# The first norm of a two-block kernel: transposed by products with a diagonal of roots, weighted piece by piece per partition

## The chip, the cores and the metric

The kernel runs on one core of a Trainium2 chip. The metric is the time of one execution in microseconds (us) of device time; lower is better. All data is fp32. Five engines work side by side, each through its own queue in order: TensorE (PE, with its weight loads shown apart as PEld), VectorE (DVE), ScalarE (ACT), GpSimd (POOL) and SyncE (SP), which here only issues DMAs.

## The reference

Two transformer blocks follow each other on x of 256 rows and 1,024 columns. The change touches only the beginning of the first layer: the first RMS norm and the projection that reads it.

```python
def rms_norm(x, w):
    y = x * lax.rsqrt(jnp.mean(x * x, axis=-1, keepdims=True) + NORM_EPS)
    return y * w

for layer in range(2):                      # first block
    h = rms_norm(x, norm_w[layer])
    proj = h @ w_in[layer]                  # q, k, v, z, q_h, f_h, i_h, g_h, two gates
    ...                                     # HGRN recurrence, windowed attention, merge
    x = x + merged @ w_out[layer]
x = rms_norm(x, final_norm_w)
...                                         # second block: attention, convolution, MoE, PLE
```

## The kernel before, in words

**Exact products from split parts.** Every fp32 factor of a projection is kept as a high part (fp32r) and a low part (the rest). `mm3` makes one product from three matmuls: high·high (L380), low·high (L381) and high·low (L382), all into one accumulator (`acc`).

**Weights.** They lie in one DRAM array, `w_all`, in units of 1 MB in the order of use, and are streamed by `Stream` into three buffers `raw`. Each unit is cut in two halves; `prepare` makes of a half its high part `whi` (ACT, L287) and its low part `wlo` (DVE, L288). A unit's DMA can go out when the buffer it takes has been split. Two units belong to the job "f", the next two to the job "i", then come those of "qh".

**The first norm.** x has two tiles of 128 rows (t = 0, 1). For each, `MeanRoot` squares the two halves on ACT (L509), adds and scales on DVE (L514, L496) and takes the root on POOL (L497). `norm_scale` (L525) multiplies x by its root and by the norm's row of weights `wb`, which a DMA has spread over all 128 partitions. `transpose_split` turns eight blocks of 128 columns on PE (L565, four to one PSUM tile `tr` of 128x512, 2 KB a partition), and `split_to` (L555) makes from each PSUM tile the high part `hTh` (ACT) and the low part `hTl` (DVE), 512 columns in one instruction each. `kk` counts the eight blocks of 128 columns of h, which are the eight steps of the contraction.

**The first projection.** `rows_job` runs "f" and then "i": each has four halves of weights, each half two steps kk, each step three matmuls of 512 columns for each row tile. That is 48 matmuls for "f", 48 for "i", 96 together, before "qh" begins. In order it does two halves for tile 0, then the same two for tile 1.

**Order.** Engines run their queues in order. A scheduler places instructions by priority when the program is built; `ahead` shifts the priority and `issue_after` ties one instruction behind another. `warm_up` issues PE products of zeros at the start (12 passes of 256 columns) and behind the first transposes (6 passes).

Of the kernel before, what the change touches and what calls it, by code (L numbers as in the profile page):

```python
# [9 lines left out]
F32 = mybir.dt.float32  # L10
F32R = mybir.dt.float32r
I32 = mybir.dt.int32
AF = mybir.ActivationFunctionType
OP = mybir.AluOpType
# [4 lines left out]
DM = 1024  # L19
KT = DM // 128  # L20
# [38 lines left out]
class Weights:  # L59


    def __init__(self):
        self.parts, self.units, self.off = [], [], 0
# [77 lines left out]
@contextmanager  # L141
def ahead(g, n):

    tc = g.tc
    tc.cur_priority -= n
    g.off += n
    yield
    g.off -= n
    tc.cur_priority += n
# [170 lines left out]
class Lazy:  # L320
# [5 lines left out]
    def __call__(self):  # L326
        if self.tile is None:
            self.tile = self.make()
        return self.tile
# [52 lines left out]
    nc.tensor.matmul(out, al, bh, start=False, stop=last)  # L382


def rows_job(g, specs, act, n, nk=KT, per=None, tile_first=False):

    hT, lT = act.hi, act.lo
    per = per or max(1, min(1024 // n, nk // 2))
    nh = nk // per

    def part(t, ps, j, hi, lo):
        s = slice(t * 128, (t + 1) * 128)
        for k in range(per):
            kk = j * per + k
            mm3(g, ps[:, :n], (hT[:, kk, s], lT[:, kk, s]), (hi[:, k], lo[:, k]), kk == 0, kk == nk - 1)

    if tile_first:
        held = {}
        for t in range(2):
            for tag, evac in specs:  # L400
                ps = g.acc.tile([128, 512], F32, tag="acc", name="acc")
                for j in range(nh):
                    while t not in act.have:
                        yield WAIT
                    if t == 0:
                        held[tag, j] = g.st.take(tag, n)
                    i, hi, lo = held[tag, j]
                    part(t, ps, j, hi, lo)
                    if t:
                        g.st.free(i)  # L410
                    if j == nh - 1:
                        with ahead(g, -10):
                            evac(t, ps)
                    yield
    else:
        for tag, evac in specs:
            while len(act.have) < 2:
                yield WAIT
            ps = [g.acc.tile([128, 512], F32, tag="acc", name="acc") for _ in range(2)]
            for jj in range(0, nh, 2):  # L420
                held = {}
                for t in range(2):
                    for j in range(jj, min(jj + 2, nh)):
                        if t == 0:
                            held[j] = g.st.take(tag, n)
                        i, hi, lo = held[j]
                        part(t, ps[t], j, hi, lo)
                        if t:
                            g.st.free(i)
                        if j == nh - 1:  # L430
                            with ahead(g, -10):
                                evac(t, ps[t])
                        yield
# [29 lines left out]
def start(g, n_keep):  # L463
    nc, h = g.nc, g.h
    g.st = Stream(g)
    g.fl = Filler(g)
    g.x = [g.keep.tile([128, DM], F32, name=f"x{t}") for t in range(2)]
    g.const = g.keep.tile([128, n_keep], F32, name="const")
    o, n = g.at["ident"]
    nc.sync.dma_start(out=g.x[0], in_=h["x"][0, 0:128, :])  # L470
    nc.scalar.dma_start(out=g.const[:, o:o + n], in_=h["const"][:, o:o + n])

    def c(name, n=0):
        o, k = g.at[name]
        return g.const[:, o:o + (n or k)]

    g.c = c
    g.half = g.keep.tile([128, 8], F32, name="half")
    nc.vector.memset(g.half, -0.5)

    g.zero = t4(g, "zero")[:, 0]
    nc.gpsimd.memset(g.zero, 0.0)
    warm_up(g, 6)


def warm_up(g, n):

    ps = g.sm.tile([128, 512], F32, tag="s", name="warm")
    for i in range(n):
        g.nc.tensor.matmul(ps[:, 0:256], g.zero[:, 0:128], g.zero, start=True, stop=True)  # L490
# [9 lines left out]
class MeanRoot:  # L500
# [5 lines left out]

    def half(self, c):
        s = slice(c * 512, (c + 1) * 512)
        self.g.nc.scalar.activation(self.scr[:, s], self.x[:, s], AF.Square, accum_out=self.ss[:, c:c + 1])  # L509

    def end(self):
        g, ss = self.g, self.ss
# [3 lines left out]
        return r  # L516


def norm_scale(g, x, wb, h, r, behind=None):

    nc = g.nc
    with g.tc.issue_after(behind.ins) if behind is not None else ExitStack():
        for c in range(2):
            s = slice(c * 512, (c + 1) * 512)
            nc.vector.scalar_tensor_tensor(h[:, s], x[:, s], r, wb[:, s], op0=OP.mult, op1=OP.mult)  # L525


def double_norm(g, x, wf, wb):
# [43 lines left out]
def normed(g, wb, hT, before):  # L572

    fl = g.fl
    h = [None] * 2
    mr = [None] * 2

    def squares(t):
        h[t] = t4(g, "h", shape=(128, DM))
        mr[t] = MeanRoot(g, g.x[t], h[t])  # L580
        for c in range(2):
            mr[t].half(c)

    def rest(t, fill, behind=None):
        norm_scale(g, g.x[t], wb, h[t], mr[t].end(), behind)
        for b in (0, 4):
            if fill:
                fl.fill((4 if b else 6) if t else 3)
            last = transpose_split(g, h[t], hT, t, b, b + 4)
        return last  # L590

    if before is None:
        for t in range(2):
            squares(t)
        last = rest(0, False)
        warm_up(g, 3)
        g.st.after(*last)
        g.st.prepare(1)
        g.st.after()
        return rest(1, False, last[1])  # L600
    for t in range(2):
        if t:
            fl.until(before)
        squares(t)
        last = rest(t, True)
    return last


def load_row(g, tag, src, n=DM):
    t = g.p.tile([128, n], F32, tag=tag, name=tag, bufs=g.nwb if tag == "wb" else 1)  # L610
    g.nc.sync.dma_start(out=t, in_=bcast(src))
    return t
# [46 lines left out]
def t2(g, name, dt=F32, shape=(128, 512)):  # L659
    return g.p.tile(list(shape), dt, tag="t2", name=name, bufs=g.nt2)  # L660


def t4(g, name, dt=F32, shape=(128, 4, 256)):
    return g.mid.tile(list(shape), dt, tag="t4", name=name, bufs=g.nt4)
# [22 lines left out]
def first_block(g):  # L687
    nc, h, p, fl = g.nc, g.h, g.p, g.fl
    g.nt2, g.nwb = 4, 2
    wb = load_row(g, "wb", h["norm_w"][0])  # L690
    nc.sync.dma_start(out=g.x[1], in_=h["x"][0, 128:256, :])
    last = None
    for l in range(2):
        last = first_layer(g, l, wb, last)
        wb = load_row(g, "wb", h["norm_w"][1] if l == 0 else h["final_norm_w"])
    return last, wb


def lower_bound(g):

    nc, h, p = g.nc, g.h, g.p
    e = t2(g, "lbe", shape=(128, 4, 128))[0:4, 0:2]
    m = g.lbr = p.tile([4, 128], F32, name="lbr")
    for l in range(2):
        nc.sync.dma_start(out=e[:, l], in_=h["lb_logits"][l].rearrange("(a d) -> a d", d=128))
    nc.vector.tensor_max(m, e[:, 0], e[:, 1])
    nc.vector.tensor_sub(e, e, m.unsqueeze(1).to_broadcast([4, 2, 128]))
    nc.scalar.activation(e, e, AF.Exp)
    nc.vector.tensor_add(m, e[:, 0], e[:, 1])
    nc.vector.reciprocal(m, m)  # L710
    nc.vector.tensor_mul(e, e, m.unsqueeze(1).to_broadcast([4, 2, 128]))
    nc.vector.tensor_add(m, e[:, 0], e[:, 1])
    nc.vector.tensor_sub(m, m, e[:, 0])
# [15 lines left out]
def first_layer(g, l, wb, last):  # L729
    nc, h, p, fl = g.nc, g.h, g.p, g.fl  # L730
# [54 lines left out]
    if l:  # L785
        jf = fl.add(rows_job(g, [("f", evac_f), ("i", evac_i)], hT, 512, tile_first=True))
    else:
        jf = fl.add(rows_job(g, [("f", evac_f), ("i", evac_i)], hT, 512))
    jqh = fl.add(cols_job(g, "qh", hT, 512, evac_qh))
    jq = fl.add(rows_job(g, [("q", evac_q)], hT, 512))  # L790
    jkv = fl.add(rows_job(g, [("kv", evac_kv)], hT, 256))
# [11 lines left out]
    fl.until(jf)  # L803
    if l == 0:
        first_setup(g)
        lower_bound(g)
    g.st.bufs, g.st.slack = 6, 1

    bT.hi, bT.lo = t4(g, "bTh", F32R), t4(g, "bTl", F32R)
# [861 lines left out]
def host_arrays(inputs):  # L1671
    inputs = {k: np.asarray(v) for k, v in inputs.items()}
    ws = lay_out(**{n: inputs[n] for n in _WEIGHTS})
    const, at, n_keep = constants()
    arrays = {n: np.ascontiguousarray(inputs[n]) for n in _SMALL}
    arrays["w_all"] = np.concatenate(ws.parts)
    arrays["const"] = const
    arrays["conv_w"] = np.ascontiguousarray(
        inputs["conv_w_2"][0].reshape(3, 4, 128).transpose(2, 0, 1).reshape(128, 12))
    route = np.concatenate([inputs["w_rg_2"][0], inputs["w_re_2"][0]], 1)  # L1680
    arrays["w_route"] = np.ascontiguousarray(route.reshape(KT, 128, 20).transpose(1, 0, 2).reshape(128, KT * 20))
    return arrays, ws.units, at, n_keep
# [15 lines left out]
```

## Time and profile before

| | |
|---|---|
| median of 3 runs | 764.17 us (762.84 to 764.51) |
| the profiled execution | 762.69 us |
| its span, from first to last instruction | 760.9 us |
| PE busy | 744.0 us (98%) |
| DVE, ACT, POOL busy | 450.1, 350.1, 21.8 us |
| TensorE clock granted by the throttle | 1.00 of full speed |

The span is what the rows of a trace cover; the execution is 1.8 us longer than it. Times inside the trace count from the span's start. PE is busy nearly all the time, so the table says only that what delays PE is what costs; where PE is not busy has to be read by stretch.

### The profile page before, as it was taken

To read this page: it belongs to the slowest core of one execution; us is meant where nothing else is said; L and a number is where in the kernel's file an instruction comes from. 1 tells how busy PE (TensorE), PEld (TensorE's weight loads), DVE (VectorE), ACT (ScalarE), POOL (GpSimd) and SP (SyncE) were. 2 spreads that over 40 slices of the span, in tenths; PEclk is the share of its full clock that TensorE was granted. 3 is DMA by queue.
4 is the path that set the end of the run, shared out by engine and by line. 5 is a ranking of instruction groups with operands and counts; after the bars stand their busy time and mean duration, and the time that the engine had idled before them with its cause. 6 is when DMAs were issued, how large, how long until landed. Compare 5 with 4: busy or idle time off the path is not lost. (4 is left out here: it accounts for less than half of the span.)

```text
span 760.9 us, 11932 instructions
## 1 busy us (share of the span) xinstructions
PE 744.0 (98%) x4878; PEld 612.0 (80%) x4878; DVE 450.1 (59%) x737; ACT 350.1 (46%) x581; POOL 21.8 (3%) x33
## 2 busy tenths in 40 slices
PE   7999999999999999999999999999999999999997
PEld 5899798999889888989997898999998753333356
DVE  6686388847477845876578668766472720102273
ACT  6771347725356304683546566554532420111242
POOL 0000000000000001000001310000000000000000
PEclk9999999999999999999999999999999999999999
DMA  8883043655066502337536351565339919999831
GB/s 303 319 293 111 1 166 112 239 202 224 15 235 230 214 1 98 124 115 273 187 146 222 127 207 56 200 234 222 122 147 376 379 31 378 417 417 416 334 111 56
DMA packets 29884, 153.33 MB, mean 202 GB/s; under 512 B 4600, under 2 KB 5632, under 8 KB 16768
## 3 DMA queue, kind: packets, MB, share of 16 engines
q1 hardware_dynamic: 29680, 152.45, 53.7%
q8 instruction: 40, 0.66, 0.3%
q14 instruction: 20, 0.16, 0.1%
q10 hardware_dynamic: 144, 0.07, 0.1%
HBM read 151.45 MB, written 1.05 MB: 200 GB/s over the span
## 5 line engine op out<-in xcount | busy, mean ns | idle before, releaser
L288 DVE TENSOR_TENSOR wlo<-raw,whi 128x1024 fp32r<-128x1024 f32 (+1 forms) x182 | 215.8, 1220 | 75.5 <-ACT whi L287 72.4
L287 ACT CAST whi<-raw 128x1024 fp32r<-128x1024 f32 (+1 forms) x182 | 181.9, 1049 | 24.5 <-DMA raw<-in_w_all_dram 21.8
L380 PE MATMUL acc<-hTh,whi 128*128 128x256 f32 x608 | 174.2, 286 | 0.0
L381 PE MATMUL acc<-hTl,whi 128*128 128x256 f32 x608 | 171.7, 282 | 0.0
L382 PE MATMUL acc<-hTh,wlo 128*128 128x256 f32 x608 | 171.3, 282 | 0.0
L380 PEld LDWEIGHTS acc<-hTh,whi 128*128 128x128 f32 x608 | 114.7, 189 | 5.1 <-issue 4.6
L381 PEld LDWEIGHTS acc<-hTl,whi 128*128 128x128 f32 x608 | 114.6, 189 | 0.2
L382 PEld LDWEIGHTS acc<-hTh,wlo 128*128 128x128 f32 x608 | 114.7, 189 | 0.0
L380 PE MATMUL acc<-whi,hTh 128*128 128x512 f32 (+2 forms) x224 | 85.0, 380 | 0.8 <-ACT whi L287 0.8
L381 PE MATMUL acc<-wlo,hTh 128*128 128x512 f32 (+2 forms) x224 | 84.0, 375 | 0.4 <-DVE wlo L288 0.4
L382 PE MATMUL acc<-whi,hTl 128*128 128x512 f32 (+2 forms) x224 | 83.8, 374 | 0.0
L1473 PE MATMUL au<-wx,hs 128*64 128x512 f32 x208 | 59.2, 597 | 0.0
L1482 DVE SCALAR_TENSOR_TENSOR hid<-hid,cs,au 128x256 f32<-128x256 f32 x8 | 3.8, 481 | 77.2 <-ACT hid L1481 77.2
L380 PEld LDWEIGHTS acc<-whi,hTh 128*128 128x128 f32 x224 | 42.2, 188 | 7.2 <-ACT whi L287 1.2
L381 PEld LDWEIGHTS acc<-wlo,hTh 128*128 128x128 f32 x224 | 42.2, 189 | 6.6 <-DVE wlo L288 0.7
L382 PEld LDWEIGHTS acc<-whi,hTl 128*128 128x128 f32 x224 | 42.2, 188 | 6.3
L380 PE MATMUL acc<-whi,mTh 128*128 128x512 f32 x96 | 38.5, 401 | 0.0
L382 PE MATMUL acc<-whi,mTl 128*128 128x512 f32 x96 | 38.0, 396 | 0.0
L381 PE MATMUL acc<-wlo,mTh 128*128 128x512 f32 x96 | 38.0, 395 | 0.0
L1473 PEld LDWEIGHTS au<-wx,hs 128*64 128x64 f32 x208 | 17.1, 136 | 23.8 <-issue 23.0
L1501 PE MATMUL y<-wx,hidT 128*64 128x512 f32 x96 | 30.4, 596 | 0.0
L922 PEld LDWEIGHTS sc<-QA,FK 128*128 128x128 f32 x192 | 27.6, 191 | 1.9 <-DVE QA L928 0.5
(331 smaller groups left out, 1222.0 us busy)
## 6 DMA issues: line engine op xcount, KB each, us to landing
raw<-in_w_all_dram SPq DMA_DIRECT2D x98, 1024.0 KB, 4.9
wx<-in_w_all_dram SPq DMA_DIRECT2D x72, 512.0 KB, 11.1
raw<-in_w_all_dram SPq DMA_DIRECT2D x2, 1040.0 KB, 4.8
wx<-in_w_all_dram SPq DMA_DIRECT2D x2, 1024.0 KB, 6.5
x<-in_x_dram SPq DMA_DIRECT2D x2, 512.0 KB, 4.9
wb<-in_norm_w_dram SPq DMA_DIRECT2D x2, 512.0 KB, 6.9
raw<-in_w_all_dram SPq DMA_DIRECT2D x2, 512.0 KB, 8.1
out_dram<-sig SPq DMA_DIRECT2D x3, 256.0 KB, 2.0
```

The lines of the kernel that those rows point to most:

```text
L287: a = g.nc.scalar.copy(hi[:, :w], raw)
L288: b = g.nc.vector.tensor_sub(lo[:, :w], raw, hi[:, :w].bitcast(F32))
L380: nc.tensor.matmul(out, ah, bh, start=first, stop=False)
L381: nc.tensor.matmul(out, ah, bl, start=False, stop=False)
L382: nc.tensor.matmul(out, al, bh, start=False, stop=last)
L922: nc.tensor.matmul(ps[:, 4 * t + a], K[:, a, ts], q2t[:, a], start=True, stop=True)
L1473: nc.tensor.matmul(hid[q][64 * i:64 * i + 64], hs[half][kk // 4][:, kk % 4, o * 64:(o + 1) * 64], w[i][k // 2][:, k % 2], start=(kk == 0), ...
L1482: nc.vector.scalar_tensor_tensor(a, a, cs[:, q:q + 1], ps[:, 256:512], op0=OP.mult, op1=OP.mult)
L1501: nc.tensor.matmul(ps[64 * i:64 * i + 64], hT[:, k, 64 * i:64 * i + 64], w[i][k][:, 0, c2], start=(k == 0), stop=(k == 1), skip_group_chec ...
```

## The change

The first norm is written anew as `first_norm`; the later norms keep `normed`.

- The row of weights is no longer spread over all partitions. Instead a host-made array of 128x8, `norm_w0`, is loaded (ACT's queue): the weight of column 128·kk + p stands in partition p, column kk.
- x of tile 0 is loaded in two DMAs of 512 columns.
- A diagonal matrix with the roots is made (L648: identity times root). PE multiplies x's blocks of 128 columns by it as ordinary fp32 products (L626), which transpose and scale by the root in one.
- `parts` makes the high and low parts, now 128 columns at a time (since the weight is a scalar per partition that differs from kk to kk): four instructions on ACT (L633) and four on DVE (L634) for each PSUM tile, before one and one.
- `split` ties one half of weights behind each group of parts, by issue order on ACT and DVE.
- `rows_job` takes `step=1` for the first job: one half for tile 0, then the same half for tile 1.
- `lower_bound` is issued earlier (`ahead(g, -60)`).

```diff
-def rows_job(g, specs, act, n, nk=KT, per=None, tile_first=False):
+def rows_job(g, specs, act, n, nk=KT, per=None, tile_first=False, step=2):
...
-            for jj in range(0, nh, 2):
+            for jj in range(0, nh, step):
                 held = {}
                 for t in range(2):
-                    for j in range(jj, min(jj + 2, nh)):
+                    for j in range(jj, min(jj + step, nh)):
...
-    nc.sync.dma_start(out=g.x[0], in_=h["x"][0, 0:128, :])
+    for c in range(2):
+        c2 = slice(c * 512, (c + 1) * 512)
+        nc.sync.dma_start(out=g.x[0][:, c2], in_=h["x"][0, 0:128, c2])
     nc.scalar.dma_start(out=g.const[:, o:o + n], in_=h["const"][:, o:o + n])
+    g.w0 = g.keep.tile([128, KT], F32, name="w0")
+    nc.scalar.dma_start(out=g.w0, in_=h["norm_w0"])
...
     if before is None:
-        for t in range(2):
-            squares(t)
-        last = rest(0, False)
-        warm_up(g, 3)
-        g.st.after(*last)
-        g.st.prepare(1)
-        g.st.after()
-        return rest(1, False, last[1])
+        return first_norm(g, hT)
...
+class Queue:
+    def __init__(self, g):
+        self.g, self.last = g, None
+
+    def __call__(self, f):
+        with self.g.tc.issue_after(self.last.ins) if self.last is not None else ExitStack():
+            self.last = f()
+        return self.last
+
+def first_norm(g, hT):
+    nc, st = g.nc, g.st
+    act, dve = Queue(g), Queue(g)
+    scr = t4(g, "h", shape=(128, DM))
+    turned = {}
+
+    def turn(t, b, by):
+        ps = turned[t, b] = g.sm.tile([128, 4, 128], F32, tag="s", name="tr")
+        for k in range(4):
+            nc.tensor.matmul(ps[:, k], g.x[t][:, (4 * b + k) * 128:(4 * b + k + 1) * 128], by, start=True, stop=True)
+
+    def parts(t, b):
+        s, ps = slice(t * 128, (t + 1) * 128), turned[t, b]
+        for k in range(4):
+            kk = 4 * b + k
+            hi, lo, w = hT.hi[:, kk, s], hT.lo[:, kk, s], g.w0[:, kk:kk + 1]
+            act(lambda: nc.scalar.activation(hi, ps[:, k], AF.Copy, scale=w))
+            dve(lambda: nc.vector.scalar_tensor_tensor(lo, ps[:, k], w, hi.bitcast(F32), op0=OP.mult, op1=OP.subtract))
+
+    def split(n):
+        st.after(act.last, dve.last)
+        st.prepare(n)
+        act.last, dve.last = st.last
+        st.after()
+
+    diag = t2(g, "diag", shape=(128, 2, 128))
+    for t in range(2):
+        mr = MeanRoot(g, g.x[t], scr)
+        for c in range(2):
+            act(lambda: mr.half(c))
+        r = mr.end()
+        dve(lambda: nc.vector.tensor_scalar(diag[:, t], g.c("ident"), r, None, op0=OP.mult))
+        turn(t, 0, diag[:, t])
+        if t == 0:
+            warm_up(g, 3)
+    parts(0, 0)
+    split(1)
+    parts(1, 0)
+    split(2)
+    with ahead(g, -12):
+        turn(0, 1, diag[:, 0])
+        parts(0, 1)
+        split(3)
+        turn(1, 1, diag[:, 1])
+        parts(1, 1)
+        split(4)
+    hT.have.update((0, 1))
+    return act.last, dve.last
...
-    wb = load_row(g, "wb", h["norm_w"][0])
+    wb = None
...
-        jf = fl.add(rows_job(g, [("f", evac_f), ("i", evac_i)], hT, 512))
+        jf = fl.add(rows_job(g, [("f", evac_f), ("i", evac_i)], hT, 512, step=1))
...
-        lower_bound(g)
+        with ahead(g, -60), g.tc.issue_after(end[0].ins), g.tc.issue_after(end[1].ins):
+            lower_bound(g)
```

What the scheduler made of it is seen in the order of the queues. First ACT, from the squares of tile 1 to the first weights; `h_98` and `h_95` are scratch for squares, `tr` are the PSUM tiles, the names in brackets are the semaphores for which an instruction waits (those of DMA lanes begin with DMAHW). Before:

```order
L509 ACTIVATE h_98,ss_99<-x1_71 128x512 [waits DMAHW3_49]
L509 ACTIVATE h_98,ss_99<-x1_71 128x512
L555 CAST hTh_92<-tr_108 128x4x128 [waits PE_49]
L555 CAST hTh_92<-tr_115 128x4x128 [waits PE_49]
L287 CAST whi_133<-raw_126 128x1024 [waits DMAHW4_49]
L287 CAST whi_191<-raw_126 128x1024 [waits DMAHW5_49]
L555 CAST hTh_92<-tr_143 128x4x128 [waits PE_49]
L555 CAST hTh_92<-tr_150 128x4x128 [waits PE_49]
```

In the changed kernel, the same stretch:

```order
L513 ACTIVATE h_95,ss_114<-x1_71 128x512 [waits DMAHW4_49,Activation_49]
L513 ACTIVATE h_95,ss_114<-x1_71 128x512 [waits Activation_49]
L633 ACTIVATE hTh_93<-tr_105,w0_76 128x128 [waits DMAHW2_49,PE_49]
L633 ACTIVATE hTh_93<-tr_105,w0_76 128x128 [waits DVE_49] x3
L287 CAST whi_142<-raw_135 128x1024 [waits DMAHW5_49]
L633 ACTIVATE hTh_93<-tr_122,w0_76 128x128 [waits PE_49]
L633 ACTIVATE hTh_93<-tr_122,w0_76 128x128 [waits DVE_49] x3
L287 CAST whi_154<-raw_135 128x1024 [waits DMAHW6_49]
L633 ACTIVATE hTh_93<-tr_158,w0_76 128x128 [waits PE_49]
L633 ACTIVATE hTh_93<-tr_158,w0_76 128x128 [waits DVE_49] x3
```

Four large instructions became sixteen small ones, a half of weights now stands between each four, and the second to fourth of each four wait for DVE.

Then DVE of the changed kernel, from the first root to the second half of weights (`rs_100` and `rs_117` are the roots of tile 0 and 1):

```order
L518 TENSOR_TENSOR rs_100<-ss_97 128x1 [waits Activation_49]
L500 TENSOR_SCALAR rs_100<-rs_100 128x1 [waits DVE_49]
L518 TENSOR_TENSOR rs_117<-ss_114 128x1 [waits Activation_49]
L500 TENSOR_SCALAR rs_117<-rs_117 128x1 [waits DVE_49]
L648 TENSOR_SCALAR diag_96<-const_72,rs_100 128x128 [waits DMAHW0_49,Pool_49]
L648 TENSOR_SCALAR diag_96<-const_72,rs_117 128x128 [waits Pool_49]
L634 SCALAR_TENSOR_TENSOR hTl_94<-tr_105,w0_76,hTh_93 128x128 [waits DMAHW2_49,Activation_49]
L634 SCALAR_TENSOR_TENSOR hTl_94<-tr_105,w0_76,hTh_93 128x128 [waits Activation_49] x3
L288 TENSOR_TENSOR wlo_143<-raw_135,whi_142 128x1024 [waits DMAHW5_49,Activation_49]
L634 SCALAR_TENSOR_TENSOR hTl_94<-tr_122,w0_76,hTh_93 128x128 [waits Activation_49] x4
L288 TENSOR_TENSOR wlo_155<-raw_135,whi_154 128x1024 [waits DMAHW6_49,Activation_49]
```

The diagonal of tile 0 stands behind the sums of tile 1's squares, and each half's `wlo` stands between two groups of four pieces.

Last SP, whose queue holds the DMAs; `raw_171` is the fourth unit of weights, and what stands ahead of it from `const_72` on is the set-up load that before stood behind the sixth unit:

```order
L266 DMA raw_140<-in_w_all_dram 128x2048 [waits DMAHW0_49]
L689 DMA pos_194<-in_positions_dram 128x2x1 [waits DMAHW1_49]
L676 DMA const_72<-in_const_dram 128x980 [waits DMAHW2_49]
L680 DMA masks_409<-in_const_dram 128x768 [waits DMAHW3_49]
L669 DMA hw0_411<-in_hgrn_norm_w_dram 128x128 [waits DMAHW4_49]
L669 DMA hw1_413<-in_hgrn_norm_w_dram 128x128 [waits DMAHW5_49]
L669 DMA sinks0_415<-in_attn_sinks_dram 128x8 [waits DMAHW6_49]
L669 DMA sinks1_417<-in_attn_sinks_dram 128x8 [waits DMAHW7_49]
L266 DMA raw_171<-in_w_all_dram 128x2048 [waits DMAHW0_49,DVE_49]
```

The set-up loads moved ahead of the fourth unit; this unit still waits for DVE, which has to finish the `wlo` of the second half before the buffer is free.

## Rows read from the trace of the kernel before

**Rows 1.** Busy time of the engines by stretch: stretch, its length, busy (count), clock, DMA

```profile
0.00:13.50 13.50, 9.50 (x35) 6.73 (x35) 5.90 (x13) 7.96 (x15) 1.89 (x15) 1.00 0.84 308
13.50:40.00 26.50, 26.49 (x133) 22.40 (x134) 19.52 (x28) 21.14 (x26) 0.00 (x0) 1.00 0.85 309
40.00:761.00 721.00, 707.97 (x4712) 582.90 (x4710) 424.73 (x698) 320.99 (x542) 19.90 (x18) 1.00 0.52 196
```

**Rows 2.** Timeline of the first 36 us: start, length, engine, line, what, [idle before]

```profile
1.17 5.14 PE L490 MATMUL warm<-zero 128*128 128x256 f32 x12 [1.17 <-POOL zero L482]
...
1.30 0.42 SPq L611 DMA_DIRECT2D wb<-in_norm_w_dram  x1
...
4.65 0.63 ACT L509 ACTIVATE h<-x 128x512 f32<-128x512 f32 x1 [2.13 <-DMA x<-in_x_dram]
...
7.87 0.63 ACT L509 ACTIVATE h<-x 128x512 f32<-128x512 f32 x1 [1.89 <-DMA x<-in_x_dram]
...
9.00 1.46 PE L490 MATMUL warm<-zero 128*128 128x256 f32 x6
...
9.11 1.05 ACT L555 CAST hTh<-tr 128x512 fp32r<-128x512 f32 x2
9.24 0.16 DVE L514 TENSOR_TENSOR rs<-ss 128x1 f32<-128x1 f32 x1 [0.79 <-ACT h L509]
9.43 0.15 DVE L496 TENSOR_SCALAR rs<-rs 128x1 f32<-128x1 f32 x1
...
11.27 0.50 PE L380 MATMUL acc<-whi,hTh 128*128 128x512 f32 x1 [0.82 <-ACT whi L287]
...
13.51 0.50 PE L381 MATMUL acc<-wlo,hTh 128*128 128x512 f32 x1 [0.42 <-DVE wlo L288]
...
14.07 0.39 PE L380 MATMUL acc<-whi,hTh 128*128 128x512 f32 x1
...
35.32 0.40 PE L382 MATMUL acc<-whi,hTl 128*128 128x512 f32 x1
```

**Rows 3.** DMA issues of the first 14 us, with the median time to landing

```profile
wb<-in_norm_w_dram SPq DMA_DIRECT2D x1, 512.0 KB, 5.2
```

**Rows 4.** Groups of ACT by shape: count | busy, mean ns of one | idle before

```profile
L287 ACT CAST whi<-raw 128x1024 fp32r<-128x1024 f32 x178 | 178.1, 1048 | 24.5 <-DMA raw<-in_w_all_dram 21.8 <-PE acc L382 2.7
...
L1076 ACT ACTIVATE P<-P,m 128x128 f32<-128x128 f32 x24 | 9.3, 390 | 0.1
...
L1481 ACT ACTIVATE hid<-au 128x256 f32<-128x256 f32 x8 | 3.1, 383 | 25.3 <-PE au L1473 25.3
...
L763 ACT COPY va<-acc 128x128 f32<-128x128 f32 x4 | 1.1, 272 | 0.0
...
L1659 ACT ACTIVATE sig<-acc,rs 128x256 f32<-128x256 f32 x2 | 0.9, 474 | 4.4 <-PE acc L382 4.4
```

**Rows 5.** The same view of DVE

```profile
L288 DVE TENSOR_TENSOR wlo<-raw,whi 128x1024 fp32r<-128x1024 f32 x178 | 211.1, 1220 | 75.4 <-ACT whi L287 72.4 <-issue 1.9 <-PE acc L381 1.0
...
L1084 DVE TENSOR_SCALAR P<-P,m 128x128 f32<-128x128 f32 x24 | 5.2, 279 | 0.1
...
L1482 DVE SCALAR_TENSOR_TENSOR hid<-hid,cs,au 128x256 f32<-128x256 f32 x8 | 3.8, 481 | 77.2 <-ACT hid L1481 77.2
...
L1365 DVE SCALAR_TENSOR_TENSOR hl<-xw,rs,hh 128x512 fp32r<-128x512 f32 x4 | 3.0, 745 | 0.0
```

**Rows 6.** One line's instructions: durations in ns, shortest/median/longest

```profile
L908 PE MATMUL sc<-qhT,FK x32: 270/273/275, 50.7 to 255.4; 128*128 128x128 f32 x32
```

**Rows 7.** Timeline where ACT and DVE both read one PSUM tile, lbp

```profile
201.53 0.59 ACT L724 COPY lb<-lbp 128x512 f32<-128x512 f32 x1 [9.16 <-PE lbp L722]
202.15 0.69 DVE L725 TENSOR_SCALAR lb<-lbp 128x512 f32<-128x512 f32 x1 [1.01 <-ACT lb L724]
```

**Rows 8.** Line L266, the weights' DMAs of the first 60 us: time to landing

```profile
DMA to landing us min/median/max: 4.8/6.1/10.3
```

More of the change, by code (lines that the diff above doesn't have):

```diff
@@ L508, in half @@
         s = slice(c * 512, (c + 1) * 512)
-        self.g.nc.scalar.activation(self.scr[:, s], self.x[:, s], AF.Square, accum_out=self.ss[:, c:c + 1])
+        return self.g.nc.scalar.activation(self.scr[:, s], self.x[:, s], AF.Square, accum_out=self.ss[:, c:c + 1])
     def end(self):
@@ L516, in end, with norm_scale @@
         return r
[L519 to L525, printed above, removed]
+def norm_scale(g, x, wb, h, r):
+    for c in range(2):
+        s = slice(c * 512, (c + 1) * 512)
+        g.nc.vector.scalar_tensor_tensor(h[:, s], x[:, s], r, wb[:, s], op0=OP.mult, op1=OP.mult)
 def double_norm(g, x, wf, wb):
@@ L582, in squares, with rest @@
             mr[t].half(c)
-    def rest(t, fill, behind=None):
-        norm_scale(g, g.x[t], wb, h[t], mr[t].end(), behind)
+    def rest(t):
+        norm_scale(g, g.x[t], wb, h[t], mr[t].end())
         for b in (0, 4):
-            if fill:
-                fl.fill((4 if b else 6) if t else 3)
+            fl.fill((4 if b else 6) if t else 3)
             last = transpose_split(g, h[t], hT, t, b, b + 4)
@@ L604, in normed @@
         squares(t)
-        last = rest(t, True)
+        last = rest(t)
     return last
+class Queue:
[29 more added lines that the diff above has]
+        mr = MeanRoot(g, g.x[t], scr)
+        for c in range(2):
+            act(lambda: mr.half(c))
[17 more added lines that the diff above has]
+    return act.last, dve.last
 def load_row(g, tag, src, n=DM):
@@ L1677, in host_arrays @@
     arrays["const"] = const
+    arrays["norm_w0"] = np.ascontiguousarray(inputs["norm_w"][0].reshape(KT, 128).T)
     arrays["conv_w"] = np.ascontiguousarray(
```

## The prediction

> **What bounds the kernel now.** I read the busy time by stretch first, because the table of totals hides where PE is not busy. In the first 13.5 us PE works 9.50 us, in the next 26.5 us it works 26.49, and in the remaining 721 it lacks 13.0 [rows 1]. So from 13.5 us on PE is the bound, and what idles later stands behind PE's own products and moves with them. A change of the first norm therefore counts by one number: when the stream of matmuls of the jobs "f" and "i" runs without gaps, compared with now.
>
> The timeline of that stretch gives the reference [rows 2]. The first of the 96 matmuls starts at 11.27, the second (L381) at 13.51, the third (L382) between, the fourth at 14.07, the 96th at 35.32. From the 4th to the 96th that is 21.25 us for 92 intervals, 0.231 us each, without a gap. The 40th, which I need below, starts at 14.07 + 36 x 0.231 = 22.39.
>
> **The start of the new norm, step by step.** The row `wb` and its 512 KB are gone. They stood ahead of x's second tile: `wb` was issued at 1.30 and took 5.2 us to land, so 6.50 [rows 2, 3], and the squares of tile 1 began, after waiting for x, at 7.87 [rows 2]. Tile 1 is still the third DMA of SP's queue (x of tile 0 is now two), but has 512 KB fewer ahead. It lands at the latest where `wb` did, 6.50, and at the earliest 7.87 - 6.50 = 1.37 us behind tile 0, whose squares began at 4.65: 6.0. I take 6.3.
>
> Tile 0 gains nothing from that. Its diagonal stands on DVE behind the sums of tile 1's squares, so both diagonals wait for tile 1. From the squares' start to the sum on DVE it takes 9.24 - 7.87 = 1.37, to the end of the scaling 9.58 - 9.24 = 0.34 [rows 2]: 8.01. The root of tile 0 on POOL lies under this. A 128x128 tensor_scalar took 0.28 [rows 5]; with a hand-over of 0.03 the first diagonal is ready at 8.32. (Hand-over: ACT's read of `lbp` ends at 202.12, DVE starts at 202.15 [rows 7].) For that to PE I take 0.06.
>
> An fp32 product is two passes. Six passes of 256 columns took 1.46 us from the first start to the last end, which is longer than its share [rows 2], so about 0.22 each and 0.11 for 128 columns; the last of a group needs 0.27 to its end [rows 6]. Four products are 7 x 0.11 + 0.27 = 1.04: the first PSUM tile is full at 9.42, and ACT starts on it at 9.45. Before, ACT began at 9.11 [rows 2]. PE goes on with the warm-up (1.3) and twelve products (2.6) until about 13.2, under the work of ACT and DVE that follows.
>
> **The parts, the term that decides.** A piece on ACT has 128 columns from PSUM and a scale per partition. A copy of 128 columns took 0.272; the scale costs 0.474 - 0.383 = 0.091 on 256 columns (L1659 against L1481) [rows 4]: 0.365. A piece on DVE, with a scalar per partition, goes by 0.481 at 256 and 0.745 at 512 columns [rows 5], so 0.264 for 256 and 0.349 at 128 columns.
>
> These pieces do not run side by side. DVE's needs ACT's high part, and in the new queue ACT's second to fourth piece each wait for DVE's piece before. The trace has the same case: L724 on ACT and L725 on DVE read one PSUM tile and write different halves of a pair, and DVE idled 1.01 us, until 0.03 after ACT had ended [rows 7]. So one step is 0.365 + 0.349 + 2 x 0.03 = 0.774.
>
> The Trainium skill bears on this (PSUM — Partial Sum Buffer, "PSUM bank collisions raise a hardware error"): two engines that touch one bank at the same time collide, two readers too, so software has to keep them apart by bank and not by address. The four pieces of 128 columns lie in one bank, so the page speaks against cutting a tile between the two engines, and [rows 7] agree. By the rule the sum is the one that follows; if pieces could overlap, it would be the first rival's.
>
> Then the weights. After the fourth piece ACT casts a half (1.05), DVE subtracts it (1.22) [rows 4, 5], and only then does DVE take the next group, which stands behind `wlo`. The first `wlo` is done at 9.45 + 3 x 0.774 + 0.365 + 1.05 + 0.03 + 1.22 = 14.44. From one `wlo` to the next it takes 0.349 for the first piece, three steps, and then 1.05 + 0.03 + 1.22, of which 0.38 lie beside the fourth piece: 3 x 0.774 + 2.27 = 4.59. The four halves of "f" are ready at 14.44, 19.03, 23.62 and 28.21. In the old kernel a half is consumed in 12 x 0.231 = 2.77, so PE starves three times.
>
> PE can issue the high·high products of a half before `wlo` (two of them, and one of "i" before the fourth), so at 28.21 it has done 39, and the 40th starts at 28.27 instead of 22.39: **5.9 us later**. From there a half costs ACT 1.05 and DVE 1.22 against PE's 2.77, and the stream has no gap.
>
> **What else moves.** The set-up loads stand ahead of the fourth unit of weights. That unit can go out only at 19.03, when `wlo` of the second half is done; a unit's DMA needed 4.8 to 10.3 us [rows 8], so it lands by 29.3, and the split adds 2.3. Its first half is wanted 23 intervals before the new 96th matmul (41.2), at 35.9: covered. The fifth unit goes out after the fourth `wlo` and the fourth unit's landing, at the latest 29.3, lands by 39.6, is split by 41.9 and is wanted at 41.4: the worst case costs 0.5. `lower_bound` and its exponent lie beside PE's full stretch, as before. `step=1` lets PE use one half for both tiles, which I have counted; in the old order PE would need two halves for tile 0 first.
>
> **Sum.** The profiled execution took 762.69, 1.8 more than its span of 760.9, and a delay of PE's stream lengthens both alike. 762.69 + 5.9 = 768.6. The median shown is 764.17, by which it would be 770.1; nothing tells which of the two the next runs follow, so I take the middle, 769.3.
>
> Bounds: pieces cannot be cheaper than the plain ones of 128 columns, 0.272 and 0.279 [rows 4, 5]. A step is then 0.61, a period 4.10, the first `wlo` ready at 13.85, the fourth at 26.15: 3.8 instead of 5.9. They cannot be dearer than those of 256 columns, 0.474 and 0.481: step 1.015, period 5.32, first at 15.27, fourth at 31.2: 8.9. The exponent's 128-column instruction at 0.390, which reads a scalar per partition too [rows 4], says that I am nearer the lower end. Tile 1's landing adds 0.3 either way.
>
> **Rivals.** *The pieces overlap* (not slower). If ACT's next piece ran beside DVE's, ACT would need 4 x 0.365 + 1.05 = 2.51 for a group and a half, DVE 4 x 0.349 + 1.22 = 2.62. The first `wlo` is ready at 13.21, the fourth at 21.07, the 40th matmul starts at 21.13 instead of 22.39: 1.3 us gained, 762.1. It decides from a period below some 2.6 us. The waits in the queue and [rows 7] speak against it; for it speaks only that before, whole tiles in different banks did overlap (two high parts in 1.05 us, with DVE behind them).
>
> *PE's clock falls.* The first twelve passes took 0.43 us each, the later six 0.24 with their end [rows 2]: 1.2 and 2.4 GHz, with a granted clock of 1.00 in both. In the new stream PE would idle some 2 us of every 4.6. Before it kept the higher level though 4.0 of the first 13.5 us were idle [rows 1], but it never paused so often. A fall in the last gap costs half of the opening's 5.14, 2.6 us more: 771.9. The Trainium skill (TensorE: Matmul & The Clock Gate, "HAM oscillation — how this bites in real kernels") describes bursts of matmuls with waits between, in which each burst starts at the lower clock; whether these waits are long enough no row here tells.
>
> *A late weight* (the fifth unit at its longest landing): 0.5 to 2 us more, 769.8 to 771.3.
>
> **Chances.** The serial pieces 0.72 (769.3; its own range by the bounds 766.5 to 773.0, from 762.69 + 3.8 and 764.17 + 8.9), the clock on top 0.13, a late weight 0.06, overlap 0.09. The first three all end slower and inside that range, so it holds over 8 in 10, and I keep it as the range. A measurement of this kernel can tell some 0.2%, 1.5 us. The overlap gives 762.1, a gain just below that; at the lower bounds it would pass it: faster 0.05, within 0.2% 0.04, slower 0.91.
>
> **What the new profile would show.** Right: ACT L633 and DVE L634 in turn, each waiting for the other, a step near 0.77; `wlo` ready about every 4.6 us; PE idle for some 2 us before L381 three times, waiting for DVE L288; the first matmul of "qh" near 41.4 instead of 35.55; no other difference later. Wrong: L633 in one run without idle, or matmuls of 0.46 us between the gaps, or PE waiting for `raw`.

## The result and the profile after

The changed kernel takes 768.45 us in the median of 7 runs (767.42 to 770.09), the kernel before in the same series 764.51 (762.42 to 767.71). The ratio is 1.006 with a 95% interval of 1.0041 to 1.0078: slower, by some 0.6%. The profiled execution took 768.05 us with a span of 766.2, against 762.69 and 760.9 before, so 5.4 and 5.3 more.

The timeline of the opening (columns as in [rows 2]) shows the new start and the turns of ACT and DVE:

```profile
6.05 0.63 ACT L513 ACTIVATE h<-x 128x512 f32<-128x512 f32 x1 [0.57 <-DMA x<-in_x_dram]
...
7.69 0.29 DVE L648 TENSOR_SCALAR diag<-const,rs 128x128 f32<-128x128 f32 x1
...
8.04 1.83 PE L626 MATMUL tr<-diag,x 128*128 128x128 f32 x8 [2.17 <-DVE diag L648]
...
9.66 2.50 PE L494 MATMUL warm<-zero 128*128 128x256 f32 x6
...
9.91 0.37 ACT L633 ACTIVATE hTh<-tr,w 128x128 fp32r<-128x128 f32 x1 [2.53 <-PE tr L626]
10.31 0.35 DVE L634 SCALAR_TENSOR_TENSOR hTl<-tr,w,hTh 128x128 fp32r<-128x128 f32 x1 [1.60 <-ACT hTh L633]
10.69 0.37 ACT L633 ACTIVATE hTh<-tr,w 128x128 fp32r<-128x128 f32 x1 [0.42 <-DVE hTl L634]
11.09 0.35 DVE L634 SCALAR_TENSOR_TENSOR hTl<-tr,w,hTh 128x128 fp32r<-128x128 f32 x1 [0.43 <-ACT hTh L633]
...
11.99 2.84 PE L626 MATMUL tr<-diag,x 128*128 128x128 f32 x24
...
13.60 1.23 DVE L288 TENSOR_TENSOR wlo<-raw,whi 128x1024 fp32r<-128x1024 f32 x1 [0.58 <-ACT whi L287]
...
14.59 0.72 PE L380 MATMUL acc<-whi,hTh 128*128 128x512 f32 x2
```

Tile 1 of x is squared at 6.05, not at 7.87 [rows 2]. But then each of the two engines stands idle for 0.42 us before its piece, and the engine named behind the arrow is always the other one: ACT starts a piece at 9.91, 10.69, 11.48 and 12.26, a step of 0.78. The first low part of a weight is ready at 13.60 + 1.23 = 14.83; the next three start 4.43 us apart, as DVE's timeline shows:

```profile
18.03 1.23 DVE L288 TENSOR_TENSOR wlo<-raw,whi 128x1024 fp32r<-128x1024 f32 x1 [0.58 <-ACT whi L287]
22.46 1.23 DVE L288 TENSOR_TENSOR wlo<-raw,whi 128x1024 fp32r<-128x1024 f32 x1 [0.58 <-ACT whi L287]
26.88 1.23 DVE L288 TENSOR_TENSOR wlo<-raw,whi 128x1024 fp32r<-128x1024 f32 x1 [0.58 <-ACT whi L287]
```

PE uses a half up in 12 x 0.231 = 2.77 us and then waits. Its timeline around the second half, and around the first matmul of "qh":

```profile
17.24 0.40 PE L382 MATMUL acc<-whi,hTl 128*128 128x512 f32 x1
18.05 0.74 PE L380 MATMUL acc<-whi,hTh 128*128 128x512 f32 x2 [0.41 <-ACT whi L287]
19.31 0.50 PE L381 MATMUL acc<-wlo,hTh 128*128 128x512 f32 x1 [0.52 <-DVE wlo L288]
...
28.19 0.47 PE L381 MATMUL acc<-wlo,hTh 128*128 128x512 f32 x1
...
41.48 0.28 PE L380 MATMUL acc<-hTh,whi 128*128 128x256 f32 x1
```

The chain of starts breaks twice for each half: 17.24 to 18.05 for the high part, then 18.05 to 19.31, two intervals' worth of work, because the low part is late. The idle times in brackets are smaller than what is lost, since a row of 0.39 covers more than its interval of 0.231. "qh" begins at 41.48 instead of 35.55: 5.93 later.

The busy time by stretch (columns as in [rows 1]):

```profile
0.00:13.50 13.50, 10.16 (x40) 8.50 (x41) 2.60 (x11) 6.40 (x15) 1.89 (x15) 0.87 0.85 311
13.50:40.00 26.50, 23.72 (x102) 17.65 (x102) 19.41 (x40) 17.83 (x29) 0.00 (x0) 1.00 0.74 265
40.00:766.20 726.20, 714.30 (x4756) 588.94 (x4754) 428.89 (x696) 327.76 (x551) 19.89 (x18) 1.00 0.52 195
```

In the second stretch PE, which idled 0.01 us before, idles 2.78. In the third it idles 11.9 instead of 13.0. And the first has something that before did not have: a granted clock of 0.87.

### The profile page after: what moved, and what is told of

It is laid out like the page before. It is cut to its first block, busy times and chain, and to the rows that moved or that the text cites. A ratio compares the mean times of both kernels' runs of the same rounds, so it can differ in the third digit from the quotient of the medians.

```text
span 766.2 us, 11983 instructions
## 1 busy us (share of the span) xinstructions
PE 748.2 (98%) x4894; PEld 615.1 (80%) x4894; DVE 450.9 (59%) x747; ACT 352.0 (46%) x592; POOL 21.8 (3%) x33
## 5 line engine op out<-in xcount | busy, mean ns | idle before, releaser
L381 PE MATMUL acc<-hTl,whi 128*128 128x256 f32 x608 | 171.7, 282 | 0.0
L381 PEld LDWEIGHTS acc<-hTl,whi 128*128 128x128 f32 x608 | 114.6, 189 | 0.2
L381 PE MATMUL acc<-wlo,hTh 128*128 128x512 f32 (+2 forms) x224 | 84.3, 376 | 1.0 <-DVE wlo L288 1.0
L381 PEld LDWEIGHTS acc<-wlo,hTh 128*128 128x128 f32 x224 | 42.2, 189 | 7.8 <-DVE wlo L288 1.8
L381 PE MATMUL acc<-wlo,mTh 128*128 128x512 f32 x96 | 38.0, 396 | 0.0
```

Source lines behind the costliest of these rows:

```text
L381: nc.tensor.matmul(out, ah, bl, start=False, stop=False)
```

## The experiments

All keep the change's diagonal products, 128x8 weights and order of loads, unless said. One thing has to be read first: x's second tile lands at another time from run to run, though its DMA stands in the same place of the queue. The landing times come from one profiled execution of each kernel, and so does the span; that execution is the fastest of its kernel's twelve in E9 and the second slowest of ten in E3. The table gives the start of tile 1's squares, the first product, the first matmul of "f" and the first of "qh", all from PE's and ACT's timelines in us, and the span of the profiled execution.

| kernel | squares of tile 1 | first product | first "f" | first "qh" | span | time against before |
|---|---|---|---|---|---|---|
| before | 7.87 | - | 11.27 | 35.55 | 760.9 | 1 |
| changed | 6.05 | 8.04 | 14.59 | 41.48 | 766.2 | 1.006 |
| E1 two loops | 7.23 | 9.22 | 14.11 | 36.40 | 762.5 | 1.0039 |
| E2 two PSUM tiles | 7.16 | 9.15 | 14.64 | 37.82 | 763.5 | 1.0003 |
| E3 whole tiles | 6.80 | 8.79 | 16.42 | 38.74 | 765.9 | 1.0012 |
| E4 longer warm-up | 7.44 | 9.43 | 14.34 | 42.16 | 767.0 | one run |
| E5 = E1 + E4 | 7.84 | 9.83 | 14.72 | 37.00 | 764.6 | 1.0031 |
| E6 diagonal early | 6.07 | 8.10 | 12.88 | 35.16 | 763.9 | 1.0018 |
| E7 step of two | 7.49 | 9.48 | 15.92 | 43.11 | 767.6 | one run |
| E8 lower_bound back | 7.60 | 9.59 | 16.14 | 43.29 | 770.3 | one run |
| E9 lower_bound ahead | 6.05 | 6.87 | 11.76 | 34.06 | 759.0 | 0.9974 |
| E10 less far ahead | 6.04 | 6.85 | 11.74 | 34.03 | 760.6 | 1.001 |
| E11 = E9 with turns | 6.96 | 6.86 | 12.85 | 40.69 | 765.4 | 1.0046 |
| E12 = E9, bound as E6 | 6.92 | 6.87 | 12.35 | 34.63 | 762.7 | 1.0011 |

**E1: the same pieces, not in turns.** ACT does its four, then DVE its four.

```diff
-        for k in range(4):
-            act(... hi_k ...); dve(... lo_k ...)
+        for k in range(4):
+            act(... hi_k ...)
+        for k in range(4):
+            dve(... lo_k ...)
```

> The same pieces and weights, but per group first ACT's four, then DVE's four; nothing is left out. Theory (the turns of ACT and DVE on one PSUM tile cost the time): ACT no longer waits for DVE; wlo comes about every 4 x 0.35 + 1.23 = 2.6 us instead of 4.43, which is under the 2.77 that PE takes for a half, so PE has no gap after its first low part. PE's stream then starts where its products end, about 14.8, and the first qh matmul comes near 14.8 + 96 x 0.231 = 37.0 instead of 41.48: about 763.6 by the profiled run's 768.05. Rival (thirty-two small instructions cost what they cost, in whatever order): period stays above 4, qh near 41.5, 768.

DVE's timeline of this kernel (its line is L636 here):

```profile
11.60 1.13 DVE L636 SCALAR_TENSOR_TENSOR hTl<-tr,w,hTh 128x128 fp32r<-128x128 f32 x4 [1.69 <-ACT hTh L633]
12.64 1.22 DVE L288 TENSOR_TENSOR wlo<-raw,whi 128x1024 fp32r<-128x1024 f32 x1
13.78 1.12 DVE L636 SCALAR_TENSOR_TENSOR hTl<-tr,w,hTh 128x128 fp32r<-128x128 f32 x4
14.83 1.21 DVE L288 TENSOR_TENSOR wlo<-raw,whi 128x1024 fp32r<-128x1024 f32 x1
```

Four pieces take 1.13 us without a gap, and the low parts come 2.2 us apart, half of 4.43. PE's waits between 13 and 45 us list nothing any more, and "qh" stands 27.18 us behind the first product instead of 33.44: 6.3 us less, of which 0.7 are the opening's clock (E4) and the rest, some 5.5, is the turns' price. The profiled span is 762.5. The median over ten runs, 766.55 (763.38 to 771.0), ratio 1.0039 (1.0012 to 1.0065), is 3 us above what I expected, and its interval overlaps that of the changed kernel, so by time alone E1 would not decide. Its executions spread with the mean granted clock: 763.38 at 1.000 and 764.33 at 0.999, but 770.57 to 771.0 at 0.993. I come back to that at E5.

**E2: in turns, but in two PSUM tiles.** Pieces 0 and 2 of a group in one, 1 and 3 in another; each tile fills 2 KB a partition.

```diff
-        ps = turned[t, b] = g.sm.tile([128, 4, 128], F32, tag="s", name="tr")
+        ps = turned[t, b] = [g.sm.tile([128, 4, 128], F32, tag="s", name="tr") for _ in range(2)]
...
-            act(... ps[:, k] ...); dve(... ps[:, k] ...)
+            act(... ps[k % 2][:, k] ...); dve(... ps[k % 2][:, k] ...)
```

> The pieces stay in turns, but pieces 0 and 2 of a group lie in one PSUM tile (bank), 1 and 3 in another; nothing is left out. Theory (the bank is what makes ACT's next piece wait for DVE's last): ACT's next piece runs beside DVE's, a group's four take about 4 x 0.40 + 0.35 = 2.0 us instead of 2.7 to 3.1, the period falls from 4.43 to 3.3 to 3.7, qh comes 2 to 3.5 us earlier, 764.5 to 766. Rival (the order by turns itself, each high part handed to DVE): step stays 0.78, period 4.4, 768.

DVE's timeline:

```profile
11.23 1.56 DVE L634 SCALAR_TENSOR_TENSOR hTl<-tr,w,hTh 128x128 fp32r<-128x128 f32 x4 [1.41 <-ACT hTh L633]
13.38 1.22 DVE L288 TENSOR_TENSOR wlo<-raw,whi 128x1024 fp32r<-128x1024 f32 x1 [0.58 <-ACT whi L287]
...
16.50 1.22 DVE L288 TENSOR_TENSOR wlo<-raw,whi 128x1024 fp32r<-128x1024 f32 x1 [0.58 <-ACT whi L287]
```

DVE's four pieces now follow each other in 1.56 us: ACT makes the next high part while DVE makes the last low part. The period is 3.12, "qh" stands 28.67 behind the first product, 4.8 us less than in the changed kernel at a similar clock of the opening (0.61 from 8 to 12 us, against 0.57), and the ratio is 1.0003 (0.998 to 1.0027). So it is not the handing over piece by piece that costs most, but that both engines' pieces lie in one PSUM tile. Within one tile ACT waits for a semaphore of DVE, so the wait that was measured is one of the program. Whether the chip would let both engines read one tile at once, no run here tells.

**E3: whole tiles.** The norm's weight is left out; ACT and DVE each make a group's 512 columns at once, as before the change.

```diff
-        for k in range(4): ...
+        act(lambda: nc.scalar.copy(hi, ps))
+        dve(lambda: nc.vector.tensor_sub(lo, ps, hi.bitcast(F32)))
```

> The norm's weight is left out, so the output is another one; a group's parts are one ACT copy and one DVE subtraction of 128x512, as in the kernel before. Theory (turns): as the two loops, qh near 37.0 and about 763.6, because PE's products set the start in both. Rival (small instructions themselves): this one alone is fast, 763.6, and the two loops stay near 768.

The period of the low parts is 1.74 (16.48, 18.22, 19.95), against 2.2 for the two loops: cutting in four, with the weight, costs 0.45 us a group, and nothing of it reaches PE, which needs 2.77. The ratio is 1.0012 (0.9992 to 1.0032). Yet "qh" comes 29.95 behind the first product, later than in E1. Three windows of the same execution (stretch, length, busy, clock, DMA) say why:

```profile
8.00:12.00 4.00, 3.21 (x12) 2.94 (x13) 1.29 (x5) 1.23 (x4) 0.55 (x1) 0.50 1.04 438
12.00:16.00 4.00, 4.00 (x24) 3.73 (x23) 1.91 (x3) 1.53 (x3) 0.00 (x0) 0.69 0.69 269
16.00:20.00 4.00, 4.00 (x22) 3.34 (x22) 3.75 (x6) 4.00 (x6) 0.00 (x0) 1.00 0.32 72
```

Products and warm-up ran at the lower clock from 8 to about 14.5 us (0.50, then 0.69 over four microseconds; 0.50 is 1.2 of 2.4 GHz), and the first matmul of "f" waited for them until 16.42. Without turns, the start is set by PE's own products.

**E4: a longer opening warm-up**, ten matmuls of zeros instead of six.

> Ten instead of six opening warm-up matmuls, so that PE works until its first products. Theory (turns decide, the opening clock is a small part): the eight product passes take near 1.04 us instead of 1.83, ACT's first piece starts near 9.45 instead of 9.91, every later wlo and qh come 0.4 to 0.5 us earlier (qh near 41.0). Rival (the lower clock at the opening is the main loss): qh 2 us earlier or more, 766 or below.

The first eight passes took 1.16 us instead of 1.83, at a granted clock of 1.00 throughout, and "qh" stands 32.73 behind the first product instead of 33.44: 0.7 us gained, as expected in kind and a little more. The span is longer all the same (767.0 against 766.2): tile 1 came 1.4 us later, twice what was gained. The opening's clock is a small part of the loss.

**E5: E1 with the longer warm-up.**

> The two loops with the ten warm-up matmuls. Theory: PE's stream again starts where the products end, about 4.9 us behind the first product, and qh about 27.2 us behind it, as in the two loops alone; but the products no longer fall to the lower clock in some executions, so the median comes down from 766.55 to that kernel's undisturbed 763.4 to 764.3: about 764.0, ratio to before 1.000. Rival (the spread of the two loops has nothing to do with the opening): median stays near 766.5, ratio 1.004.

The expected gain did not come. The granted clock is now 0.996 to 1.000 in all twelve executions and the longest takes 768.35 instead of 771.0, but the median is 766.05, ratio 1.0031 (1.0016 to 1.0045). In the profile "qh" comes 27.17 behind the first product, as in E1, but that product waited until 9.83 for tile 1, and PE idles 1.2 us in the 20 us behind 37.0, most of it waiting for qhT and FK, two operands of the next stage (E6). So E1's spread seems to have been the opening's clock in part; its level was not.

**E6: E5, and tile 0 does not wait for tile 1.** In the change DVE makes tile 0's diagonal behind the sums of tile 1. Here the sums of tile 1 are ordered behind it.

```diff
-        r = mr.end()
+        with g.tc.issue_after(dve.last.ins) if t else ExitStack():
+            r = mr.end()
```

> As e5, and tile 1's sums are ordered behind tile 0's diagonal, so that tile 0's products no longer wait for tile 1 of x. Theory (with the turns gone, what bounds the start is PE's thirty-two passes of products behind tile 1's diagonal and the first low part, both now about 2 us earlier): stream starts about 12.0 us, 2.0 us earlier than e5, qh about 34.3 against 35.55 of before; some 762.5 and below before, ratio 0.998. Rival (ACT's squares of tile 1 and the landing of raw hold the start): stream starts as in e5, ratio 1.000.

The first diagonal is made at 6.53 instead of 7.69, but the ten warm-ups run until 8.26 and hold the products back to 8.10. "qh" comes at 35.16, 0.4 earlier than before the change, yet the ratio is 1.0018 (1.0005 to 1.003). PE's waits between 34 and 60 us show where a part of it goes:

```profile
PE sc L970 <- ACT FK L963: 0.9, 2, 0.6
PE sc L970 <- DVE qhT L745: 0.8, 1, 0.8
```

**E7 and E8: two other parts of the change undone in the changed kernel.** E7 takes two halves of a weight per tile again (`step=2`), E8 puts `lower_bound` where it stood.

> The changed kernel with two halves of a weight per tile, as before the change. Theory: parts still come every 4.43 us; tile 0 then waits for its second group of parts (done near 22.5) and PE's gaps gather in one of about 4 us, but tile 1 then has all it needs: the 49th matmul comes 0.4 us later than in the changed kernel, 768.5. Rival (the step of one is what keeps the loss small): qh 2.5 us or more later, 770.5 or above.

> The changed kernel with lower_bound where it stood before the change. Theory (costed at nothing, since it lies beside PE's full stretch): qh at the same place, 41.5 to 42.2, total within 1 us of 768.05. Rival (the moved loads and DVE work delay the parts): qh 1 us or more earlier, below 767.

From the first product to "qh" they take 33.63 and 33.70 us, the changed kernel 33.44: neither part is worth more than 0.3 us there. Both totals are later than expected (769.44 and 772.06, one run each). Tile 1 came 1.4 and 1.55 us later in them, and in E8 a stretch of 100 us far behind, from 603 to 703, had a granted clock of 0.98, some 2 us (2% of 100). With that and the later "qh" (1.8 us) nearly all of the 4.1 us by which E8's span is longer is accounted for, but one run each settles no difference under 1 us.

**E9 and E10: E6 with the short warm-up, and `lower_bound` out of the way.** In E6 the scheduler had set its exponent (0.42 us) with a table load (1.28 us) on ACT in front of the last FK and qhT.

```diff
-        with ahead(g, -60), g.tc.issue_after(end[0].ins), g.tc.issue_after(end[1].ins):
+        with ahead(g, 300), g.tc.issue_after(end[0].ins), g.tc.issue_after(end[1].ins):
             lower_bound(g)
```

(E10 has 100 instead of 300.)

> As e6, but with six opening warm-up matmuls again (its ten ran until 8.26 us and held tile 0's products back, whose diagonal was ready at 6.8), and with lower_bound's loads and its exponent ordered far ahead, so that its table load no longer stands in ACT before FK and qhT. Theory: the stream starts at about 11.7 us instead of 12.9 and the 1.75 us in which PE waited for FK and qhT behind 35.16 go: 763.9 of span - 1.2 - 1.75 = 761.0, ratio to before 0.999. Rival (what is won at the start is waited for later, since DVE and ACT are no earlier there): ratio stays near 1.002.

> As e9, with lower_bound ordered less far ahead: its exponent stands beside that of the rope tables, before the first evacuation. Theory: the same start near 11.7 us, one table load more on ACT than e9 beside PE's full stretch, so the same time as e9 within 1 us, ratio 0.999. Rival as in e9: 1.002.

PE's timeline of E9:

```profile
6.87 1.16 PE L626 MATMUL tr<-diag,x 128*128 128x128 f32 x8 [0.59 <-DVE diag L651]
7.87 1.46 PE L494 MATMUL warm<-zero 128*128 128x256 f32 x6
9.16 2.84 PE L626 MATMUL tr<-diag,x 128*128 128x128 f32 x24
11.76 0.48 PE L380 MATMUL acc<-whi,hTh 128*128 128x512 f32 x1
12.08 0.40 PE L381 MATMUL acc<-wlo,hTh 128*128 128x512 f32 x1
...
34.06 0.28 PE L380 MATMUL acc<-hTh,whi 128*128 128x256 f32 x1
```

E9 has a median of 762.26 (760.79 to 765.37) against 762.93 for before, ratio 0.9974 (0.9952 to 0.9995): it is well ahead of the changed kernel and just ahead of the one before. "f" starts at 11.76 and runs without a gap. E10 starts at the same place but is not within 1 us of E9 as expected: 1.001 (0.9994 to 1.0026), with 0.5 us of PE idle between 40 and 60 us where E9 has none. The rest of that difference stays open.

**E11: the turns put back into E9**, and nothing else.

> The kernel of e9 with ACT's and DVE's pieces in turns again, and nothing else changed. Theory (the turns alone cost the time): first piece at 8.07 as in e9, low parts every 4.43 us, the fourth done at 8.07 + (28.11 - 9.91) = 26.3; the 40th matmul then starts near 26.3 instead of e9's 11.76 + 39 x 0.231 = 20.8, PE waits for wlo and whi again: 5.5 us more, about 764.5 of span, some 767 to 768 in the median, ratio to before 1.004 to 1.006. Rival (e9 is fast by its earlier start and its order, the turns cost little there): within 1.5 us of e9.

DVE's timeline, and the first matmul of "qh" in PE's:

```profile
12.83 1.22 DVE L288 TENSOR_TENSOR wlo<-raw,whi 128x1024 fp32r<-128x1024 f32 x1 [0.58 <-ACT whi L287]
...
17.26 1.23 DVE L288 TENSOR_TENSOR wlo<-raw,whi 128x1024 fp32r<-128x1024 f32 x1 [0.58 <-DMA hw<-in_hgrn_norm_w_dram]
...
40.69 0.28 PE L380 MATMUL acc<-hTh,whi 128*128 128x256 f32 x1
```

The period is 4.43 again, and PE waits for `whi` (2.2 us) and `wlo` (1.5 us). "qh" comes 6.6 us later than in E9. Some 0.9 of that are the later tile 1, whose squares start at 6.96 instead of 6.05: DVE's first piece stands behind tile 1's diagonal in its queue, and each further step waits for it. That leaves some 5.7 for the turns. The span is 6.4 longer, the median 5.2. The ratio is 1.0046 (1.0032 to 1.0059). Its interval and that of E9 do not touch: one edit, the order of the same thirty-two instructions, moves the time by 0.7%, some 5.5 us. This pair decides the case.

**E12: E9 with `lower_bound` as in E6.**

> The kernel of e9 with lower_bound where e6 has it, so that its table load stands before the last FK and qhT. Theory (the order of ACT around FK costs PE a wait of its own): the stream starts at 11.7 as in e9, PE waits 1.7 us for FK and qhT behind 34, median about 1.7 to 3 us above e9, ratio 1.000. Rival (the wait is noise of that one profile): as e9, ratio 0.997.

PE's waits between 34 and 60 us:

```profile
PE sc L970 <- DVE qhT L745: 0.8, 1, 0.8
PE sc L970 <- ACT FK L963: 0.8, 2, 0.5
```

Between 60 and 130 us PE also waits for the softmax's P. The first line is E12's; the second is all that E9 waits for that product behind 33 us:

```profile
PE PTp L1152 <- DVE P L1146: 1.6, 1, 1.6
PE PTp L1152 <- DVE m L1127: 0.6, 2, 0.3
```

The median is 764.77, ratio 1.0011 (0.9996 to 1.0026), 2.5 us above E9. The profiled span is 3.7 longer, of which 0.6 are the later tile 1 ("qh" at 34.63 instead of 34.06). So the waits are real: the place of `lower_bound` took back what the new norm had won at the start. All of `lower_bound` moves between the two, its loads and DVE's part too, so what the table load alone cost is not shown.

## Why the prediction was right

The forecast was 769.3 us, slower, from serial pieces; the median came out at 768.45. Step by step:

- **Tile 1's landing** (6.3, between 6.0 and 6.5): its squares began at 6.05. In other kernels with the same DMAs ahead of it they began as late as 7.84, outside the bounds and no earlier than with `wb` (7.87). That it fell inside here was luck, and that dropping `wb` brings tile 1 forward is not shown.
- **ACT's first piece** (9.45): 9.91. The first product came 0.34 earlier than I had it (8.04 instead of 8.38), but the eight passes took 1.83 instead of 1.04, at a granted clock of 0.57 from 8 to 12 us (0.87 over the stretch to 13.5). This term was mis-sized. PE's products also ended near 14.8 instead of 13.2, which cost little, since the first low part was ready at 14.83.
- **A step of 0.774**: 0.78. The groups by shape give the two pieces as I had them, 0.365 and 0.349:

```profile
L633 ACT ACTIVATE hTh<-tr,w 128x128 fp32r<-128x128 f32 x16 | 5.9, 368 | 10.2 <-DVE hTl L634 7.6 <-PE tr L626 2.5
```
```profile
L634 DVE SCALAR_TENSOR_TENSOR hTl<-tr,w,hTh 128x128 fp32r<-128x128 f32 x16 | 5.6, 350 | 6.8 <-ACT hTh L633 6.8
```

- **The period** (4.59): 4.43, because an engine's next instruction starts about 0.1 us before the row of the one before it ends (a piece at 12.26 of 0.37, the cast behind it at 12.53), twice in a period. With the late first piece the fourth low part was done at 28.11, against 28.21: by luck the two errors nearly cancelled.
- **The 40th matmul** (28.27): 28.19. **"qh"** (near 41.4): 41.48.
- **PE's gaps** (some 2 us before L381, three times): the place was right and the shape not. A gap comes in two parts: the first is 0.58 before the high part (17.24 to 18.05, less one interval) and 0.8 around the low part (18.05 to 19.31, less two). The second is 4.43 - 2.77 = 1.66 in all, the other two some 1.4.
- **No other difference later**: not quite. Of the 5.93 us at "qh" 5.3 are left in the span. Before, PE waited 1.2 us for the softmax's P (L1084) between 60 and 130 us; after, only the other wait of that stretch is left, as long as before:

```profile
PE tr L567 <- DVE o L1041: 1.0, 1, 1.0
```

The wait for P is also gone in E4, E7 and E8, where PE comes late as well, in E8 with `lower_bound` where it stood before. E1, with `lower_bound` as in the changed kernel but an earlier PE, waits 1.6 us. So a chain on DVE that was late for PE is less so when PE comes later; this rests on one profile of each kernel. Moving `lower_bound` far ahead shortens the wait too, whenever PE comes: E9 and E10 reach "qh" first of all and wait 0.3 us there.

Of the rivals, **overlap** is out: pieces in one PSUM tile never ran side by side, and they did at once in E2, in two tiles. The Trainium skill's rule (PSUM — Partial Sum Buffer, "PSUM bank collisions raise a hardware error") is that two engines are to be kept apart by bank. This trace agrees: the pieces in one tile follow each other at 0.78, and E2's four in two tiles take 1.56. The price that I gave this rival, 762.1, was too low: PE's products were to end at about 13.2, and 39 matmuls of 0.231 behind them reach to 22.2, not 21.13. E1, whose pieces hold PE up no more, starts "f" 4.9 us behind its first product, when its own products are done. **The clock in the gaps**: it did not fall there. Behind each gap the matmuls follow at 0.23 us and the stretch from 13.5 to 40 has a granted clock of 1.00. The Trainium skill's description of bursts that start at the lower clock (TensorE: Matmul & The Clock Gate, "HAM oscillation — how this bites in real kernels") is not what these gaps of under 1 us show. The clock fell in the opening instead, where I had not looked for it. **A late weight**: PE's waits from 13 to 60 us name only `whi` and `wlo` of the first five halves, in four and two cases; none lies behind 28 us.

The total came out lower than the middle I took. That it came so near is in part luck: between the profiled executions the loss is 5.4 us, but between the medians of the series only 3.9 (by the ratio's interval 3.1 to 6.0), against the 5.9 of the forecast. The kernel before spread over 5.3 us in that series, the changed one over 2.7; why is open.

## What to carry to other kernels

Two engines that took turns on one PSUM tile went at the sum of their times here (0.78 us a step), whatever their shares of busy time say; let one finish its pieces before the other begins, or give the pieces two tiles. A part of 128 columns per partition weight costs little (0.45 us a group here) as long as its engine has slack against the one that bounds. And when an opening gets shorter, look at what the scheduler then sets in front of the next stage: the place of `lower_bound`, whose exponent and table load stood in front of the last FK and qhT, took back the whole gain of E9.

## What was not expected of the hardware

The granted clock of the opening varies between kernels, and by the mean clock of E1's executions (0.993 to 1.000) it may do so between executions too. From 8 to 12 us it was 1.00 before the change and in E1, although PE idled 2.56 us ahead of E1's products. It was 0.57 in the changed kernel behind 2.17 us of idling, 0.61, 0.66 and 0.73 in E2, E7 and E8 behind about 3, and 0.50 in E3 behind 3.27. With ten warm-up matmuls it was 1.00 in E4, E5 and E6, and with six in E9 to E12, where PE idled 1.25 us or less. So the idle time ahead of the products does not alone say when it falls; what else does stays open.

The same DMA of 512 KB, third in the same queue and issued at 1.76 or 1.77 us in all the profiles with the change, let tile 1's squares begin near 6.05 in four of them and at 7.84 in another. That moves the start of these kernels by up to 1.8 us, as much as several of the effects looked for here, and only the time from the first product shows them.
